# A hybrid attention block on one core: new order with PSUM turns, shared memory and transfers in the planner, and another opening

## The chip, the cores and the metric

The kernel runs on one core of a Trainium2 chip. The metric is the device time of one execution in microseconds (us). A run is one execution; the time of a kernel is the median of its runs.

The engines are PE (TensorE: matrix products and transposes), DVE (VectorE), ACT (ScalarE), POOL (GpSimd) and SP, which issues transfers. Each engine runs its instructions in the order in which they were issued and waits at an instruction whose data isn't there, so the order of the program on each engine decides who waits for whom. PSUM is the memory into which PE writes its results; SBUF is the other memory on the core.

## The reference

One layer, 1024 tokens by 1024 channels, float32. Shift, scale and gate (six vectors of 1024) come from a vector c.

```python
c_act = jax.nn.silu(c)
mod = (c_act @ w_ada[l] + b_ada[l])[:, None, :]
shift1, scale1, gate1, shift2, scale2, gate2 = jnp.split(mod, 6, axis=-1)
h = rms_norm(x, norm1_w[l]) * (1.0 + scale1) + shift1
x = x + gate1 * hybrid_mixer(h, ...)
h = rms_norm(x, norm2_w[l]) * (1.0 + scale2) + shift2
x = x + gate2 * swiglu(h, w_gate[l], w_up[l], w_down[l])
return rms_norm(x, norm_f_w)
```

The mixer projects h by w_in to q, k, v, z of four heads of 128, two columns a and b per head, and the three parts of a short gated convolution. q, k and v pass a causal convolution of width 4 and SiLU; a gated delta rule in chunks of 64 tokens then needs, per chunk, decays from a, the products of k with k and q, a triangular inverse of 64x64, and a chain over the chunks that carries a 128x128 state. The results, gated by z, and the short convolution's go through w_out. SwiGLU has 2816 inner channels.

## The kernel before

**Tiling.** The channels stand on the 128 partitions in eight blocks (k = 0 to 7); the tokens are split into two halves of 512 (hf = 0, 1). Each float32 operand of a large product is split into a high and a low part, and a product is three passes (high by high, low by high, high by low) of 128x128 weights against 512 columns. These are the rows `acc` of the profile. `h` is the normalised input (high and low), `u` a split block of w_in, `whl` one of the first blocks of w_in.

**The opening** works on the first half of the tokens. x is loaded in four tiles (`x0`). The sums of squares are taken by ACT, the roots give `rs`; tiles 0 and 1 are scaled by rs on DVE, while for tiles 2 and 3 the transpose of the first block multiplies by a diagonal `dgx` of rs instead, on PE. `load0` loads, block by block, a block of w_ada's scale and shift (`wa`, 512 KB each) and a block of w_in (`wr`). `sums0` has DVE multiply a block of `wa` with c (`c_bc`, spread over the partitions by PE's products `ps`) and sum along the row; ACT makes the columns `s1c` and `b1c` from the sums. `xh0` transposes x (`tr`); `h_make` writes h's high part from PSUM by ACT, once more in full as `hf`, and DVE subtracts for the low part. `wsplit0` splits `wr`, and `acc0` runs the first products into six PSUM banks. `HEAT` counts dummy products (`heat`), placed ahead of these to keep PE at work: 4 and 12 in the code ahead of the planner and 16 in `acc0`.

**The planner.** From `load0` on, everything up to the middle of the kernel is written as tasks, each a thread of the program that builds the kernel. Class `Sim` runs them: each operation asks for a start, `cost` prices it, `ready` says when its data and places are free, `MARGIN`, `HOLD`, `BIAS` and the table `PR` of priorities weigh, and the operation that can start first is issued next. So the planner's opinion of costs, start times (`T_START`, `PIPE0`) and waits writes the order on each engine. All operations issued through it carry one line of the profile, L452 (`either`); those issued in plain order carry L87 on PE and L88 elsewhere.

**Tasks of the delta rule.** `ab_phase(hf)` makes PE's products `ab`, a copy of them to SBUF (`raw<-ab`), PE's transposes `abt`, then by small DVE and ACT steps the decays, and PE's products `G`. `decays` and `stage_a` make per head the exponentials (`L`, `at`, `WQ`; loaded as `WQ<-g_scr`), PE's transposes `kT` and `qT`, and the products `kk` and `qk`. `gdn(hf)` then solves the triangles on DVE (pairs of operations on tiles `A` and `qs`), copies blocks of the result from `xbd` to `DD` (a tile of tag `qs`) and `XA` (tag `A`), transposes `DD` on DVE, and spawns `merge`, whose first products on PE are `P<-qs,L`, followed by `Q<-qs,A`. The chain has products V, K, A and O per chunk; `output` norms and gates them and PE transposes them (`y<-ident,u`).

**Memory.** The first half's pools (x, s) are given back and used again as pool gp for the delta rule's tiles; b1 is given back and used as x2 for the residual input; `xbd` is used twice. `h1_work` makes the second half's h from the old memory; the tiles of gp wait for it. A first use of such memory waits for the last use of the old. `load_y` (`y0`, `y1`) reloads the mixer's outputs (`raw<-y_scr`) and splits them to `WQ` for w_out's products (`o`). `coordinator` opens the pools and loads the eight tiles of x2; tiles 2 to 7 were either issued at once or held back (`held`) until w_out's weights were loaded.

After the planner's end comes a part in hand-written order: the rest of w_out, SwiGLU (`acc`, L87) and its down projection (`dn`), with the final norm. The change leaves it alone.

Of the kernel before, what the change touches and what calls it, by code (L numbers as in the profile page):

```python
# [9 lines left out]
F32 = mybir.dt.float32  # L10
# [8 lines left out]
HEAT = (4, 12, 16)  # L19
# [32 lines left out]
def kernel(  # L52
# [6 lines left out]
    w_mod: bass.AP,  # L59
    w_in0: bass.AP,  # L60
# [197 lines left out]
    mods = sp.tile([P, 2 * KB], F32, name="mods", tag="mods")  # L258
# [13 lines left out]
    for i, t in enumerate(x0):  # L272
# [4 lines left out]
        seq("dve", DVE.reciprocal(rs, s1))  # L277
        if i < 2:
            seq("dve", DVE.tensor_scalar(t, t, rs, None, ALU.mult))
        elif i == 2:  # L280
            seq("dve", DVE.scalar_tensor_tensor(nb1, bac[:, 8:16], 1.0, n1c, ALU.add, ALU.mult))
            seq("dve", DVE.tensor_scalar(dgx[i], ident, rs, None, ALU.mult))
        else:
            seq("act", ACT.activation(dgx[i], ident, AF.Copy, scale=rs))
# [21 lines left out]
    class Sim:  # L306
        ENG = {"pe": "pe", "dve": "dve", "act": "act", "pool": "pool", "sp": "sp"}

        def __init__(self, chain_, start):
# [5 lines left out]
            self.log, self.idle = [], {}  # L315
# [4 lines left out]
        def own(self, t, res, i, t0=0.0):  # L320
            self.owner[t.tensor.name] = (res, i)
            if t0:
                self.acc[t.tensor.name] = [[0, P, 0, 1 << 30, t0, True, None]]
# [50 lines left out]

        def cost(self, eng, op, a, k):
            outs, ins = [], []
# [21 lines left out]
            elif eng == "act":  # L398
                big = max([n] + [v.free_size() for v in ins])
                busy = 0.15 + (0.1 if hasattr(k.get("scale"), "tensor") else 0.0) + big * 0.0007 + (0.19 if "accum_out" in k else 0.0)  # L400
# [4 lines left out]
            elif eng == "pool":  # L405
                busy = 1.1 if op == "tensor_tensor" else 0.1 + n * 0.0009 if op == "memset" else 0.65 if n >= 256 else 0.5
                lat = busy + 0.15
            else:
# [6 lines left out]
                else:  # L415
                    busy = 0.08 + big * 0.00104 + (0.05 if op == "scalar_tensor_tensor" else 0.0)
# [5 lines left out]
        def ready(self, eng, outs, ins):  # L422
            t = 0.0
            for w, aps in ((True, outs), (False, ins)):
                for ap in aps:
                    name, p0, p1, f0, f1, dram = self.region(ap)
                    for a in self.acc.get(name, ()):
                        if (w or a[5]) and a[0] < p1 and p0 < a[1] and a[2] < f1 and f0 < a[3]:
                            if eng == "pe" and a[6] == "pe" or dram and w or eng == "dma" and w and a[5] and a[6] == "dma":
                                continue  # L430
# [66 lines left out]
        def run(self):  # L497
            while True:
# [25 lines left out]
                if lat is None:  # L524
                    run_ = min(n_ for n_ in (ap.ap[-1][1] * 4 for ap in outs + ins))
                    self.pipe = max(t + DMA_T[0], self.pipe) + outs[0].nbytes() / (150e3 if run_ <= 128 else 290e3 if run_ <= 1024 else 380e3)
                    end = rd = self.pipe + DMA_T[1]
                else:
# [24 lines left out]
    for t, at in [(x0[0], 8.9), (x0[1], 9.8), (x0[2], 7.4), (x0[3], 8.4), (dgx[2], 10.2), (dgx[3], 11.1), (rs0, 10.7)] + [(cols_a, 5.0), (nb1, 9.7), (c_act, 4.0), (c_bc, 7.2)]:  # L553
# [58 lines left out]

    def load0():
        for k in range(KB):
            t = wa[k] = was.tile(wap, [P, 2, D], F32, "wa")
            for s_ in (1, 0):
                dma(t[:, s_], w_mod[k, :, s_])
# [8 lines left out]
    def sums0():  # L626
        cb = c_bc.rearrange("p a b c -> p (a b c)")
        for k in range(KB):
# [3 lines left out]
            for s_, col in ((1, s1c), (0, b1c)):  # L632
                r = mods[:, 2 * k + s_:2 * k + s_ + 1]
                DVE.scalar_tensor_tensor(t[:, s_], t[:, s_], 1.0, cb, ALU.mult, ALU.mult, accum_out=r)
                if s_:
                    ACT.activation(s1c[:, k:k + 1], r, AF.Identity, bias=nb1[:, k:k + 1], scale=n1c[:, k:k + 1])
                else:
                    ACT.activation(b1c[:, k:k + 1], r, AF.Identity, bias=bac[:, k:k + 1])
            free(t)
            done.add(("cols", k))  # L640
# [8 lines left out]
    def xh0():  # L649
        for k in range(KB):  # L650
# [4 lines left out]
            for i in range(4):  # L655
                if k == 0 and i > 1:
# [6 lines left out]
            h = h_slot(k, 0)  # L663
            h_make(k, h, ps, h_hi)
            H[k][0] = h
# [3 lines left out]
    def h_make(k, h, ps, first=None):  # L669
        hf = hfs.tile(sp, [P, HT], F32, "hf")  # L670
        ACT.activation(h[:, 0, :], ps, AF.Identity, bias=b1c[:, k:k + 1], scale=s1c[:, k:k + 1])
# [8 lines left out]
        DVE.tensor_tensor(h[:, 1, :], hf, h[:, 0, :].bitcast(F32), ALU.subtract)  # L680
        free(hf)

    def wsplit0():
        for k in range(KB):
# [4 lines left out]
            w_hi[k] = u  # L689
            DVE.tensor_tensor(u[:, 1, :], wr[k], u[:, 0, :].bitcast(F32), ALU.subtract)  # L690
# [153 lines left out]
    h1_left = list(range(KB))  # L844

    def h1_work():
        sim.wait(lambda: "x1" in done)
        while h1_left:
# [6 lines left out]
            free(hf)  # L855
            H[k][1] = h
# [140 lines left out]
    held, n_wout = [], [0]  # L997

    def ev_o(ps, m):
        sim.wait(lambda: ("x2", m) in done and "g1" in done)  # L1000
# [202 lines left out]
    def gdn(hf):  # L1203
# [40 lines left out]
        DVE.transpose(flat(DD[:, 1]), flat(DD[:, 0]))  # L1244
# [100 lines left out]
    def w_unit(k, ch, take, out_):  # L1345
# [3 lines left out]
        if n_wout[0] == 2 * KB:  # L1349
            done.add("wout")  # L1350
            for kw, m in held:
                seq("sp", nc.sync.dma_start(**kw))
                done.add(("x2", m))
# [28 lines left out]
    def take_lx(n):  # L1382
        def take():
            sim.wait(lambda: all(("uw", 1, h) in done for h in heads))
            if len(xbd) == 1:
                xbd.append(gp.tile([P, 4, HT], F32R, name="wu", tag="xbd", bufs=1))
            return gt("L", (P, HT), F32R), xbd[1][:, n, :]
        return take

    def take_wq():  # L1390
        t = gt("WQ", (P, 2, HT), F32R)
# [20 lines left out]
    def y1():  # L1412
        sim.wait(lambda: ("chain", 1) in done)
# [1228 lines left out]
```

## Time and profile before

| | us |
|---|---|
| median of 3 runs | 1144.19 (1143.35 to 1146.99) |
| the profiled execution | 1145.62 |
| its span | 1143.8 |
| first large product of PE | 15.71 |
| PE busy | 1126.6 |
| DVE busy | 948.6 |
| ACT busy | 612.1 |
| POOL busy | 99.3 |

A row of the waits view names the waiting engine, its operation, the operation that ended last before it, then the sum of the waits in us, their number and the longest. A row of the timeline has start, duration, engine, line, operation, output <- inputs, shapes, and in brackets the idle time of the engine before it with what ended it. Neighbouring equal instructions are gathered in one row (xN). A float32 product of PE is recorded as two passes. In a row of the windows stand the stretch, its length, and the busy time of PE, weight loads, DVE, ACT and POOL, then PE's granted clock, the share of the DMA engines and GB/s.

### The profile page before, as it was taken

What the parts mean: (1) busy time and instruction counts of PE and PEld (TensorE: products, weight loads), DVE (VectorE), ACT (ScalarE), POOL (GpSimd) and SP (SyncE); (2) the same over time, 40 slices, a digit from 0 to 9 for tenths busy, and PEclk for the clock granted to TensorE, in tenths of its full rate; (3) what the DMA queues carried; (4) which work ended last, traced back from release to release, by engine and by line L of the source; (5) the groups of instructions that cost most, each with busy time, mean ns of one, the idle gap of its engine ahead of it and who ended that gap; (6) DMA issues with size and microseconds to landing.
All of it is one profiled execution on the core that took longest, in us unless ns stands there. A gap on an engine that the chain in (4) does not pass through costs nothing.

```text
span 1143.8 us, 17102 instructions
## 1 busy us (share of the span) xinstructions
PE 1126.6 (98%) x5660; PEld 951.2 (83%) x5660; DVE 948.6 (83%) x1909; ACT 612.1 (54%) x1372; POOL 99.3 (9%) x150
## 2 busy tenths in 40 slices
PE   9998999999999999999999999999999999999997
PEld 7887888898888897888888888888888888888885
DVE  7798879889989856699988998878888886689976
ACT  7686863649733643255544544545454476454344
POOL 0010100101100201000010010101010000000302
PEclk9999999999999999999999999999999999999999
DMA  9933256655355472440367667876677599669933
GB/s 367 353 102 102 79 171 192 177 180 183 116 180 174 159 279 68 74 148 19 139 181 210 171 187 177 233 197 162 183 207 200 138 329 362 206 177 355 289 136 147
DMA packets 164978, 214.65 MB, mean 188 GB/s; under 512 B 52589, under 2 KB 81305, under 8 KB 164889
## 3 DMA queue, kind: packets, MB, share of 16 engines
q1 hardware_dynamic: 155832, 198.69, 53.4%
q0 software_dynamic: 7712, 14.42, 8.0%
q8 instruction: 44, 0.72, 0.3%
q10 hardware_dynamic: 1344, 0.46, 0.2%
q14 instruction: 46, 0.37, 0.1%
HBM read 163.94 MB, written 60.58 MB: 196 GB/s over the span
## 4 chain that ended last, share of the span: by engine, by line
PE 90%; ACT 3%; DVE 3%; DMA 1%; issue 1%; POOL 0%; SPq 0%; ACTq 0%; DVEq 0%
PE acc L87 36%; PE acc L452 24%; PE dn L87 16%; PE o L87 4%; PE o L452 3%; DVE xo L88 1%; PE O L452 1%; PE P L452 1%; PE Q L452 1%; PE V L452 1%; PE qk L452 1%; DMA raw<-y_scr 1%; PE K L452 1%; PE A L452 1%; ACT L L452 1%
## 5 line engine op out<-in xcount | busy, mean ns | idle before, releaser
L452 PE MATMUL acc<-h,u 128*128 128x512 f32 x1200 | 293.6, 396 | 0.0
L452 PEld LDWEIGHTS acc<-h,u 128*128 128x128 f32 x1200 | 220.4, 188 | 42.4
L87 PE MATMUL acc<-h,hl 128*128 128x512 f32 (+1 forms) x540 | 109.1, 353 | 0.1
L87 PEld LDWEIGHTS acc<-h,hl 128*128 128x128 f32 x540 | 90.3, 189 | 15.1 <-issue 0.5
L87 PE MATMUL acc<-h,u 128*128 128x512 f32 (+1 forms) x516 | 100.4, 345 | 0.0
L87 PE MATMUL acc<-T,hl 128*128 128x512 f32 x408 | 97.6, 391 | 0.3 <-DVE T L88 0.3
L87 PEld LDWEIGHTS acc<-h,u 128*128 128x128 f32 x516 | 84.7, 189 | 12.6
L87 PE MATMUL acc<-T,u 128*128 128x512 f32 x384 | 91.2, 390 | 0.0
L87 PE MATMUL dn<-h,h 128*128 128x512 f32 x396 | 90.7, 389 | 0.0
L87 PEld LDWEIGHTS acc<-T,hl 128*128 128x128 f32 x408 | 75.2, 188 | 15.8 <-DVE T L88 0.8
L87 PEld LDWEIGHTS dn<-h,h 128*128 128x128 f32 x396 | 74.4, 188 | 15.4
L87 PEld LDWEIGHTS acc<-T,u 128*128 128x128 f32 x384 | 71.0, 188 | 14.1
L452 ACT CAST u<-raw 128x512 fp32r<-128x512 f32 x68 | 41.9, 619 | 53.9 <-PE acc L452 46.5
L452 DVE TENSOR_TENSOR u<-raw,u 128x512 fp32r<-128x512 f32 x82 | 56.6, 692 | 6.4 <-ACT u L452 5.8
L88 ACT COPY L<-acc 128x256 f32<-128x256 f32 x68 | 25.3, 372 | 64.4 <-PE acc L87 64.0
L88 ACT CAST h<-rw 128x512 fp32r<-128x512 f32 x60 | 35.1, 619 | 40.8 <-PE dn L87 26.3
L88 DVE TENSOR_TENSOR xo<-xo,dn 128x512 f32<-128x512 f32 x66 | 44.9, 684 | 14.1 <-PE dn L87 13.6
L452 DVE SCALAR_TENSOR_TENSOR cv<-pr,cols_a,cv 128x512 f32<-128x512 f32 x72 | 53.0, 749 | 1.5 <-ACT cv L452 1.3
L88 DVE TENSOR_TENSOR h<-rw,h 128x512 fp32r<-128x512 f32 x60 | 39.7, 687 | 15.6 <-ACT h L88 15.6
L452 DVE SCALAR_TENSOR_TENSOR raw<-raw,cb 128x512 f32<-128x512 f32 x64 | 43.8, 686 | 4.3 <-DMA raw<-in_w_mod_dram 3.9
L88 DVE TENSOR_TENSOR cc<-cc,acc 128x512 f32<-128x512 f32 x66 | 41.3, 646 | 4.9 <-PE acc L87 4.9
L88 ACT COPY cc<-acc 128x512 f32<-128x512 f32 x64 | 35.2, 585 | 19.0 <-PE acc L87 19.0
(399 smaller groups left out, 2193.0 us busy)
## 6 DMA issues: line engine op xcount, KB each, us to landing
raw<-in_w_in_dram SPq DMA_DIRECT2D x82, 256.0 KB, 3.4
am_scr<-cc SPq DMA_DIRECT2D x75, 256.0 KB, 2.2
raw<-in_w_mod_dram SPq DMA_DIRECT2D x64, 256.0 KB, 3.1
rw<-am_scr SPq DMA_DIRECT2D x53, 256.0 KB, 5.3
R<-in_w_gate_dram SPq DMA_DIRECT2D x22, 512.0 KB, 5.1
R<-in_w_up_dram SPq DMA_DIRECT2D x22, 512.0 KB, 5.9
rw<-bm SPq DMA_DIRECT2D x43, 256.0 KB, 5.3
wa<-in_w_mod_dram SPq DMA_DIRECT2D x16, 512.0 KB, 9.3
```

The source lines that it names most:

```text
L87: return call(*a, **k)
L88: ins = call(*a, **k)
L452: ins = call(*a, **k)
```

## The change

**Opening.** A new input `w_sc0` has the first block's scale weights in w_ada's own layout (512 KB), loaded in plain order right behind x. Eight products of 128x1 on PE (`sc0`, task `scale0`) sum them against c; ACT makes `s1c` of block 0 from PSUM. DVE's reduction of that block and its transfer in `load0` are gone. The first block's shift is loaded and reduced in two halves of 512. Tile 1 of x is scaled by ACT instead of DVE; `dgx` of tile 3 is made by DVE instead of ACT. The first block's h-high is written in two halves, columns 256 to 511 by DVE, then 0 to 255 by ACT; its low part is a task of its own that waits for the reduction of block 1. HEAT goes from (4, 12, 16) to (4, 4, 14).

**Planner.** `ready` lets accesses of different engines to one PSUM bank take turns, and no longer waits for an engine's own earlier write. A transfer's issue waits for the landing of the eighth before it. New costs for strided operands, POOL, ACT. MARGIN of PE is 1.0 (was 0.6). `gone` says when the old memory of gp, x2 and xbd is free.

**Tasks.** `take_wq` waits for the second chain, `y1` for w_out's weights; tiles 2 to 7 of x2 wait for w_out's weights or for the output product of their turn. In `gdn` the transpose of DD is issued ahead of POOL's copies to XA.

```diff
-HEAT = (4, 12, 16)
+HEAT = (4, 4, 14)
-T_START = (8.6, 10.5, 11.1, 2.9, 2.9)
-PIPE0 = 8.25
+T_START = (8.6, 10.05, 11.7, 2.9, 3.4)
+PIPE0 = 9.2
-MARGIN = dict(pe=0.6)
+MARGIN = dict(pe=1.0)
...
+    wsc0 = xp.tile([P, D], F32, name=nm("wsc0"), tag="x", bufs=8)
...
+    seq("sp", SP.dma_start(out=wsc0, in_=w_sc0))
...
+                        if ap.space == PSUM and a[6] not in (eng, None):
+                            t = max(t, a[4])
+                            continue
...
-                at = way[2] = self.ready("dma" if lat is None else eng, outs, ins) + MARGIN.get(eng, 0.0)
+                at = way[2] = max(self.ready("dma" if lat is None else eng, outs, ins) + MARGIN.get(eng, 0.0), 0.0 if lat else self.landed[-8])
...
+    def scale0():
+        ps = bank(chb, "sc0")
+        for kk in range(KB):
+            mm(ps[:, 0:1], wsc0[:, kk * P:(kk + 1) * P], c_act[:, kk:kk + 1], kk == 0, kk == KB - 1)
+        ACT.activation(s1c[:, 0:1], ps[:, 0:1], AF.Identity, bias=nb1[:, 0:1], scale=n1c[:, 0:1])
+        free(ps)
+        done.add("scale0")
...
+            if k == 0:
+                a, b = slice(0, 256), slice(256, HT)
+                DVE.tensor_scalar(h[:, 0, b], ps[:, b], s1c[:, 0:1], b1c[:, 0:1], ALU.mult, ALU.add)
+                done.add("hi0")
+                ACT.activation(h[:, 0, a], ps[:, a], AF.Identity, bias=b1c[:, 0:1], scale=s1c[:, 0:1])
...
+        DVE.transpose(flat(DD[:, 1]), flat(DD[:, 0]))
         for p in range(2):
             for c in range(2):
                 q, m, r = 64 * c + 32 - 32 * p, Q_AT[p, c], 64 * c
                 POOL.tensor_copy(XA[q:q + 32, :, m:m + 32], xbd[0][r:r + 32, p::2, r:r + 32])
-        DVE.transpose(flat(DD[:, 1]), flat(DD[:, 0]))
...
     def take_wq():
+        sim.wait(lambda: ("chain", 1) in done)
...
     def y1():
-        sim.wait(lambda: ("chain", 1) in done)
+        sim.wait(lambda: "wout" in done)
...
+        left = sim.gone(x1t + h1_t)
+        for res in GP.values():
+            res.slots = [(max(t0, left), i) for t0, i in res.slots]
...
-            if i < 2 or "wout" in done:
-                dma(x2[m], x_t[m])
-                done.add(("x2", m))
-            else:
-                sim.op("sp", "dma_start", lambda **kw: held.append((kw, m)) or [], (), dict(out=x2[m], in_=x_t[m]))
+            if i > 1:
+                sim.wait(lambda: "wout" in done or len(begun) >= i)
+            dma(x2[m], x_t[m])
+            done.add(("x2", m))
```

The order on three engines at three places. First PE from its start to the first large products, before (x is a tile of the input, tr the transposed first block, ps the spread of c):

```order
L87 MATMUL ps_206<-raw_204,ones 128x512
L87 MATMUL heat<-ident,ones 128x128 x12
L452 MATMUL heat<-ident,ones 128x128 x5
L452 MATMUL tr_272<-ident,x_184 128x128
L452 MATMUL heat<-ident,ones 128x128 x3
L452 MATMUL tr_272<-ident,x_185 128x128
L452 MATMUL heat<-ident,ones 128x128
L452 MATMUL tr_272<-dgx_228,x_186 128x128
L452 MATMUL heat<-ident,ones 128x128 x3
L452 MATMUL tr_272<-dgx_229,x_187 128x128
L452 MATMUL heat<-ident,ones 128x128 x4
L452 MATMUL acc_252<-h_0_110_316,whl_278 128x512
```

The same place after the change:

```order
L88 MATMUL ps_208<-raw_206,ones 128x512
L88 MATMUL heat<-ident,ones 128x128 x4
L468 MATMUL heat<-ident,ones 128x128 x8
L468 MATMUL tr_265<-ident,x_184 128x128
L468 MATMUL heat<-ident,ones 128x128 x3
L468 MATMUL sc_103_264<-c_act,wsc_85_188 128x1 x8
L468 MATMUL tr_265<-ident,x_185 128x128
L468 MATMUL tr_265<-dgx_222,x_186 128x128
L468 MATMUL tr_265<-dgx_223,x_187 128x128
L468 MATMUL heat<-ident,ones 128x128 x3
L468 MATMUL acc_244<-h_0_112_315,whl_271 128x512
```

Seventeen heats stand ahead of the first transpose before and twelve after; the products of the scale stand between the first transpose and the second, and the other transposes follow without heats between them.

Second, ACT at the second half's ab, before (WQ and L are the first exponentials of the decays, u a split weight):

```order
L452 ACTIVATE h_1_275_1178<-hf_1179,b1c 128x512
L452 ACTIVATE h_1_271_1156<-hf_1157,b1c 128x512
L452 CAST u_1217<-raw_1194 128x512
L452 ACT_TABLE_LOAD
L452 ACTIVATE WQ_1254<-WQ_1254 128x512
L452 ACTIVATE L_1246<-L_1246,G_1090 128x128
L452 COPY raw_1284<-ab_1236 128x512
```

And after:

```order
L468 CAST u_1192<-raw_1167 128x512
L468 ACTIVATE h_1_277_1180<-hf_1181,b1c 128x512
L468 COPY ch_1194<-acc_1135 128x512
L468 ACTIVATE vT_1206<-cv_1158 128x512
L468 COPY raw_1274<-ab_1229 128x512
L468 ACT_TABLE_LOAD
L468 ACTIVATE WQ_1247<-WQ_1247 128x512
```

The copy of ab has moved from behind the table load and two exponentials to ahead of them. On PE ten products stand between the last ab and the four abt after the change, eight before; G follows forty-four products later than before.

Third, DVE ahead of the second half's P, before (qs is the tile that is transposed, the others are weight splits, a reduction of w_ada and a convolution):

```order
L452 TENSOR_TENSOR h_0_803_4136<-raw_4130,h_0_803_4136 128x512
L452 TENSOR_TENSOR cv_4163<-acc_4152,cv_4163 128x512
L452 COPY qs_4212<-xbd 32x256
L452 TENSOR_TENSOR u_4215<-raw_4171,u_4215 128x512
L452 SCALAR_TENSOR_TENSOR raw_4146,msum<-raw_4146,cb_1827 128x512
L452 TENSOR_TENSOR h_0_812_4198<-raw_4190,h_0_812_4198 128x512
L452 STREAM_TRANSPOSE qs_4212<-qs_4212 128x256
```

And after:

```order
L468 STREAM_TRANSPOSE turn<-A_3711 64x512
L468 TENSOR_TENSOR u_4185<-raw_4147,u_4185 128x512
L468 SCALAR_TENSOR_TENSOR cv_4169<-ch_4102,cols_a,cv_4169 128x512
L468 TENSOR_TENSOR h_0_804_4137<-raw_4130,h_0_804_4137 128x512
L468 TENSOR_TENSOR cv_4169<-acc_4159,cv_4169 128x512
L468 TENSOR_TENSOR u_4208<-raw_4189,u_4208 128x512
L468 TENSOR_TENSOR h_0_806_4145<-raw_4139,h_0_806_4145 128x512
L468 STREAM_TRANSPOSE qs_4223<-qs_4223 128x256
```

DVE's own copy into qs is gone (all four copies are on ACT). From the last kk to P, PE has 243 products in the first half after the change and 250 before, and 261 against 266 in the second.

More of the change, by code (lines that the diff above doesn't have):

```diff
@@ L59 @@
     w_mod: bass.AP,
+    w_sc0: bass.AP,
     w_in0: bass.AP,
@@ L282 @@
             seq("dve", DVE.tensor_scalar(dgx[i], ident, rs, None, ALU.mult))
-        else:
-            seq("act", ACT.activation(dgx[i], ident, AF.Copy, scale=rs))
+        elif i == 3:
+            seq("act", ACT.activation(x0[1], x0[1], AF.Copy, scale=rs0[:, 1:2]))
     accs = {m: psp.tile([P, HT], F32, name=nm("acc"), tag=f"b{i}") for i, m in enumerate(heads01)}
@@ L373, in region, with gone @@
             return name, p0, p0 + dims[0][1], lo, hi + 1, ap.space == bass.MemoryType.DRAM
+        def gone(self, aps):
+            return max([a[4] for ap in aps for a in self.acc.get(ap.tensor.name, ())] + [self.now])
         def cost(self, eng, op, a, k):
+            apart = lambda ap, n: n >= 256 and ap.space != PSUM and abs(ap.ap[-1][0]) > 1 and ap.ap[-1][1] > 1
             outs, ins = [], []
@@ L399, in cost @@
                 big = max([n] + [v.free_size() for v in ins])
-                busy = 0.15 + (0.1 if hasattr(k.get("scale"), "tensor") else 0.0) + big * 0.0007 + (0.19 if "accum_out" in k else 0.0)
+                busy = 0.15 + 0.09 * sum(hasattr(k.get(n_), "tensor") for n_ in ("scale", "bias")) + big * 0.0007
+                busy += (0.06 if n <= P else 0.19) if "accum_out" in k else 0.3 if apart(ins[0], n) else 0.0
                 lat = busy + 0.25
@@ L415, in cost @@
                 else:
-                    busy = 0.08 + big * 0.00104 + (0.05 if op == "scalar_tensor_tensor" else 0.0)
+                    busy = 0.08 + big * 0.00104 + (0.05 if op in ("scalar_tensor_tensor", "tensor_scalar") else 0.0)
+                if op == "transpose" and apart(ins[0], n):
+                    busy += n * 0.00104
                 if "accum_out" in k:
@@ L527, in run @@
                     end = rd = self.pipe + DMA_T[1]
+                    self.landed.append(end)
                 else:
@@ L631, in sums0 @@
             t = wa[k]
[L632 to L638, printed above, removed]
+            made = []
+            for s_ in (1, 0) if k else (0,):
+                for c in halves_of(k):
+                    r = mods[:, 2 * k + s_:2 * k + s_ + 1] if c.stop == D else mods[:, 2 * KB:2 * KB + 1]
+                    DVE.scalar_tensor_tensor(t[:, s_, c], t[:, s_, c], 1.0, cb[:, c], ALU.mult, ALU.mult, accum_out=r)
+                    made.append(r)
+            done.add(("sum", k))
+            if k:
+                ACT.activation(s1c[:, k:k + 1], made.pop(0), AF.Identity, bias=nb1[:, k:k + 1], scale=n1c[:, k:k + 1])
+            add = bac[:, k:k + 1]
+            for r in made:
+                to = b1c[:, k:k + 1] if r is made[-1] else mods[:, 2 * KB + 1:2 * KB + 2]
+                ACT.activation(to, r, AF.Identity, bias=add)
+                add = to
             free(t)
+            sim.wait(lambda: "scale0" in done)
             done.add(("cols", k))
@@ L655, in xh0 @@
             for i in range(4):
+                if k == 0 and i == 3:
+                    sim.wait(lambda: "dgx3" in done)
                 if k == 0 and i > 1:
@@ L670, in h_make @@
         hf = hfs.tile(sp, [P, HT], F32, "hf")
-        ACT.activation(h[:, 0, :], ps, AF.Identity, bias=b1c[:, k:k + 1], scale=s1c[:, k:k + 1])
+        if k:
+            ACT.activation(h[:, 0, :], ps, AF.Identity, bias=b1c[:, k:k + 1], scale=s1c[:, k:k + 1])
         if first is not None:
@@ L679, in h_make, with low @@
         free(ps)
-        DVE.tensor_tensor(h[:, 1, :], hf, h[:, 0, :].bitcast(F32), ALU.subtract)
-        free(hf)
+        def low():
+            if k == 0:
+                sim.wait(lambda: ("sum", 1) in done)
+            DVE.tensor_tensor(h[:, 1, :], hf, h[:, 0, :].bitcast(F32), ALU.subtract)
+            free(hf)
+            H[k][0] = h
+        if k == 0:
+            sim.spawn(low, 0.2)
+        else:
+            low()
     def wsplit0():
@@ L1386, in take @@
                 xbd.append(gp.tile([P, 4, HT], F32R, name="wu", tag="xbd", bufs=1))
+                sim.acc[xbd[1].tensor.name] = [[0, P, 0, 1 << 30, sim.gone(xbd[:1]), True, None]]
             return gt("L", (P, HT), F32R), xbd[1][:, n, :]
```

48 lines of the change are left out of this document (31 added, 17 removed).

## The prediction

> **What bounds the kernel now.** I read the page's parts 1 and 2 first, then the waits of TensorE (PE), then windows, then the timeline at each wait.
>
> ```profile
> PE 1126.6 (98%) x5660; PEld 951.2 (83%) x5660; DVE 948.6 (83%) x1909; ACT 612.1 (54%) x1372; POOL 99.3 (9%) x150
> PEclk9999999999999999999999999999999999999999
> ```
> PE is busy 98% of the 1143.8 us span at full granted clock. No other engine comes near, so only time in which PE stands idle can be won, or work taken from it. The waits view lists that idle time by releaser (total, times, longest):
>
> ```profile
> PE abt L452 <- ACT raw L452: 3.6, 2, 3.4
> PE P L452 <- DVE qs L452: 1.7, 1, 1.7
> PE heat L87 <- POOL ident masks.py:199: 1.4, 1, 1.4
> PE y L452 <- DVE u L452: 1.2, 2, 1.0
> PE G L452 <- ACT jk L452: 0.7, 1, 0.7
> PE ps L87 <- DVE raw L88: 0.7, 1, 0.7
> ```
> The windows (length, PE busy, PEld, DVE, ACT, POOL busy) say in which stage it lies:
>
> ```profile
> 15.70:111.00 95.30, 94.24 (x430) 76.81 (x430) 82.61 (x172) 71.26 (x122) 8.09 (x11) 1.00 0.61 218
> 111.00:139.00 28.00, 24.47 (x139) 20.40 (x140) 23.07 (x80) 25.81 (x89) 2.85 (x6) 1.00 0.31 95
> 139.00:400.00 261.00, 259.31 (x1385) 221.61 (x1384) 230.20 (x624) 147.23 (x436) 28.20 (x45) 1.00 0.54 167
> 400.00:560.00 160.00, 158.38 (x764) 130.75 (x763) 118.97 (x209) 68.94 (x140) 5.92 (x5) 1.00 0.40 119
> 560.00:1114.00 554.00, 554.00 (x2778) 472.65 (x2776) 464.38 (x779) 276.36 (x535) 44.64 (x56) 1.00 0.74 215
> ```
> Length less PE busy is 1.06, 3.53, 1.69, 1.62 and 0: 7.9 us between the first product at 15.7 and 1114. That is the most that new waits and orders can win there. Of it the waits view names abt 3.6 + P 1.7 + y 1.2 + G 0.7 = 7.2. The second half (560 on), which the change leaves alone, has nothing to win.
>
> **The change part by part.** (Line numbers are those of before.)
>
> *Opening.* PE's rows there with DVE's reduction (wa) and ACT's h, then the nearest ones for what is new (the last five: 128x1 products; DVE and ACT reading one PSUM tile, 128 columns each; ACT at 256 columns):
>
> ```profile
> 11.20 1.28 PE L452 MATMUL heat<-ident,ones 128*128 128x128 f32 x10
> 12.12 1.22 DVE L452 SCALAR_TENSOR_TENSOR wa<-wa,c_bc 128x1024 f32<-128x1024 f32 x1
> 12.32 0.27 PE L452 MATMUL tr<-ident,x 128*128 128x128 f32 x1
> 12.43 0.83 PE L452 MATMUL heat<-ident,ones 128*128 128x128 f32 x6
> 14.32 0.39 PE L452 MATMUL tr<-dgx,x 128*128 128x128 f32 x2
> 14.81 0.78 ACT L452 ACTIVATE h<-tr,b1c,s1c 128x512 fp32r<-128x512 f32 x1 [1.13 <-PE tr L452]
> 15.71 1.17 PE L452 MATMUL acc<-h,whl 128*128 128x512 f32 x4
> 470.26 0.79 PE ss L87 x8
> 155.63 0.35 DVE L452 TENSOR_SCALAR u<-vT,bv 128x128 f32<-128x128 f32 x1 [0.53 <-ACT u L452]
> 156.01 0.37 ACT L452 ACTIVATE u<-vT,bv 128x128 f32<-128x128 f32 x1 [0.42 <-DVE u L452]
> 156.41 0.35 DVE L452 TENSOR_SCALAR u<-vT,bv 128x128 f32<-128x128 f32 x1 [0.43 <-ACT u L452]
> L88 ACT COPY L<-acc 128x256 f32<-128x256 f32 x68 | 25.3, 372 | 64.4 <-PE acc L87 64.0
> ```
> A heat is two passes of 0.11 us. Ten heats fewer are 2.2 us of PE time, but they fill time in which PE would wait. The chain: the first transpose can start at 11.20 instead of 12.32, where five heats stood. Behind it three heats (0.67) and eight 128x1 products; "ss" is four such (eight passes) in 0.79, so 1.58. Then three transposes of five passes, 0.55: the last ends its start-to-start at 11.20 + 0.11 + 0.67 + 1.58 + 0.55 = 14.1, against 14.54 before. Half of h-high by DVE and half by ACT follow. The vT rows show the two engines at one tile by turns, each waiting for the other; the new order has the same, ACT's half waiting for DVE's. By turns: DVE 256 columns is above 0.35 (128 columns), about 0.46; ACT 256 is above 0.37 (the plain copy), about 0.50; 0.96 against the 0.78 of the one ACT pass. The first product comes 0.4 earlier and 0.2 later: about 0.2 won; I take 0.1, since the next products need the second block at the old time. Bounds: 0.9 won (if the halves lay side by side and all three heats were dead time) to 0.3 lost (sc0 at heat price, 1.79, and both halves 0.05 dearer). DVE's 1.22 us reduction of the scale and its DMA go, hidden work either way.
>
> The Trainium skill ("PSUM — Partial Sum Buffer", "PSUM bank collisions raise a hardware error") says that two engines must not touch one bank and partition quadrant at once, ACT with VectorE included, so they have to be kept apart; the vT rows agree. It speaks against halving this eviction: without it the halves would end 0.46 sooner, near the upper bound.
>
> *The wait of abt, second half.*
>
> ```profile
> 104.49 1.42 DVE L452 SCALAR_TENSOR_TENSOR h<-hf,b1c,h 128x512 fp32r<-128x512 f32 x2 [0.88 <-ACT h L452]
> 106.06 3.31 DMA WQ<-g_scr
> 110.85 1.28 ACT L452 ACT_TABLE_LOAD   x1 [5.27 <-DVE at L452]
> 112.97 0.56 ACT L452 COPY raw<-ab 128x512 f32<-128x512 f32 x1
> 113.59 0.66 PE L452 MATMUL abt<-ident,raw 128*128 128x128 f32 x4 [3.41 <-ACT raw L452]
> 373.66 5.60 PE L452 MATMUL acc<-h,u 128*128 128x512 f32 x24
> ```
> PE needs ab transposed; ACT's copy raw<-ab stands behind a table load and two exponentials, and these wait for a load of decays that is issued only at 106.06, when h1_work's last DVE operation has freed the memory. In the new order the copy stands ahead of the table load, needing ab alone, and PE has 10 products (0.23 each: 5.60 by 24) in place of 8 before abt: 2.3 us of cover against the copy's 0.56. The 3.4 goes; of the first half's abt (the other 0.2) too, as its copy moves to DVE under 16 products instead of 11. G moves 44 products later, 10 us: its 0.7 goes. What comes due next is the same stage: ACT is 25.81 busy of 28 there, 92%. The new order asks for the transposed q 0.7 to 2.8 us later than the old, so I put new small waits at 0.5 to 1 us, 0.8.
>
> *P.* The transpose qs of both halves, ahead of P:
>
> ```profile
> 208.17 0.43 DVE L452 STREAM_TRANSPOSE qs<-qs 128x256 f32<-128x256 f32 x1
> 209.15 1.95 PE L452 MATMUL P<-qs,L 128*128 128x128 f32 x16
> 377.67 0.44 DVE L452 COPY qs<-xbd 32x256 f32<-32x256 f32 x1
> 380.46 0.43 DVE L452 STREAM_TRANSPOSE qs<-qs 128x256 f32<-128x256 f32 x1
> 380.95 2.05 PE L452 MATMUL P<-qs,L 128*128 128x128 f32 x16 [1.69 <-DVE qs L452]
> ```
> In the second half qs is complete at 378.11 but transposed at 380.46, behind three DVE operations. The new order puts all four copies on ACT and the transpose right behind: 2.35 earlier. But from the last kk (which feeds the solve) to P PE now has 261 products against 266, 1.15 us less; of 1.69 there remains about 0.3 (1.69 - 2.35 + 1.15 = 0.5, less 0.2 as a copy leaves DVE). In the first half no wait stands in the trace, slack 209.15 - 208.60 = 0.55; 243 products against 250 take 1.6 away, the transpose comes 0.7 to 1.4 earlier: a new wait of 0 to 1.5, taken at 0.4. P wins 1.7 - 0.3 - 0.4 = 1.0.
>
> *y.*
> ```profile
> 424.90 1.83 SPq L452 DMA_DIRECT2D raw<-y_scr  x4
> 431.36 0.43 DVE L452 CAST WQ<-raw 128x512 fp32r<-128x512 f32 x1 [2.06 <-DMA raw<-y_scr]
> 435.68 0.66 PE L452 MATMUL y<-ident,u 128*128 128x128 f32 x4 [1.05 <-DVE u L452]
> ```
> DVE's norm of the last outputs stood behind a cast that waited for these loads, which SP issued behind eight loads of x2. Now six of the eight wait for w_out, two of the four y loads are issued ahead, and 30 output products stand before y. The 1.2 goes. x2 is needed only from the first output products on; a late tile costs DVE, not PE, while PSUM has free banks.
>
> Sum: opening 0.1, abt 3.6, G 0.7, stage A -0.8, P 1.0, y 1.2: 5.8 us. The profiled execution took 1145.62 (span and 1.82 around it), 1.43 over the median of 1144.19; from it 1139.8, from the median **1138.4**. About 0.3% (3.4 us) is what a measurement of this kernel can tell from no change: faster means below 1140.8, slower above 1147.6.
>
> **The rivals.**
> *A: the wait only moves.* ACT paces stage A (111 to 139), so PE, freed from abt, stands later at kk, kT or qT. For it: 92% ACT. Against: PE's order has other products to fill, and DVE (23.07 of 28) can help. ACT then starts earlier by 0 to 0.7 (one of the two h operations of 104.49 is gone from that place), taken at 0.5; with 0.2 from the first abt, the stage gives 0.7 instead of 3.5. Sum 0.7 + 0.1 + 1.0 + 1.2 = 3.0: 1141.2, within 0.3%.
> *B: slower, the solve becomes the bound.* Both halves have fewer products between kk and P, and the triangular solve between is a chain of dependent DVE operations with others set between them. If the new mixture delays it, PE waits at P one for one. Slower by 0.3% takes 5.8 + 3.4 = 9.2 us over two solves: some seven more foreign DVE operations of 0.7 (the two h above: 1.42) in each. The order shows 28 between in the first, as before, which speaks against.
> *C: the opening does not do what it says.* The scale's products or the two turns cost what the reduction gave: -0.3 instead of 0.1, 1138.8; still faster.
> *D: the clock cools.* With ten heats fewer, PE may fall back to the slow passes with which it began:
>
> ```profile
> 7.79 3.57 PE L87 MATMUL heat<-ident,ones 128*128 128x128 f32 x24
> ```
> These 24 passes take 3.57 where 24 at 0.11 are 2.6: about the first seven or eight ran at 0.21, until 9.4, so PE was slow for some 5 us after the ps products began at 4.22. A second such stretch at half speed costs 2.6: gain 3.2, 1141.0. Against: the abt row after 3.41 idle is 0.66 long, the y row after 1.05 idle the same, so that much idle did not cool it, and the opening has under 1 us by the chain above. The Trainium skill ("TensorE: Matmul & The Clock Gate", Part 1) halves the clock after an idle window of about 3.4 us; the abt row, at that length, shows no halving.
>
> **How the numbers follow.** Forecast 0.52; A 0.24; B 0.08; C 0.08; D 0.02; other small waits that leave it within 0.3% 0.02, other slower 0.04. Faster: 0.52 + 0.08 = 0.60. Same: 0.24 + 0.02 + 0.02 = 0.28. Slower: 0.08 + 0.04 = 0.12. Low end: all of the 7.9 and 0.9 of the opening, 8.8: 1135.4, rounded down to 1135.0. High end: A with the stage at 0.2, P at 1.7 - 0.3 - 1.5 = -0.1, the opening at -0.3, y at 1.2: 1.0, 1143.2; with a part of the slower cases 1144.0.
>
> **What would show it.** In the waits of PE the rows abt, G and y gone; P at most 0.8; no new row over 1 us (kk, kT or qT: then A; a P row of several us: B). ACT's copy raw<-ab right behind ab's last product, ahead of the table load. First product at 15.5 to 15.75, the eight sc0 products in 1.4 to 1.8. The window 111 to 139 with under 1.5 us of PE idle. Wrong it would be if the idle sum from first product to the tail stays over 5 us, or the tail past 1114 grows.

## The result and the profile after

| kernel | median, us | before beside it | ratio, 95% interval |
|---|---|---|---|
| after | 1135.48 (1135.19 to 1136.64, 6 runs) | 1144.85 (6 runs) | 0.9918 [0.9905, 0.9930] |
| after, run again (e9) | 1135.59 (1134.91 to 1136.11, 5 runs) | 1143.73 (9 runs) | 0.9925 [0.9911, 0.9939] |

The change makes the kernel faster by 8.1 to 9.4 us, where 5.8 was forecast. The profiled execution of after took 1135.19 with a span of 1133.4; that is 10.4 under before's profiled one, about 1 more than the medians differ by.

The waits of PE in after (what waits, on what, then the sum in us, the number, the longest):

```profile
core 0 of [0], span 1133.4 us
PE heat L88 <- POOL eps_c L89: 1.5, 1, 1.5
PE acc L468 <- ACT h L468: 0.9, 1, 0.9
PE sT L468 <- POOL rs L468: 0.7, 1, 0.7
PE sc L468 <- DMA wsc<-in_w_sc_dram: 0.5, 1, 0.5
PE acc L88 <- DVE T L89: 0.3, 1, 0.3
```

All of abt, P, y and G are gone. Three rows are new: sc and the first acc lie in the opening, sT (the transposed row norms, at 62.2) is in the middle. The windows of after, over the same stages (stretch, its length, PE busy, then the other engines):

```profile
14.26:111.00 96.74, 96.08 (x440) 78.59 (x441) 87.81 (x185) 71.40 (x122) 7.78 (x11) 1.00 0.63 227
111.00:139.00 28.00, 28.00 (x160) 24.01 (x159) 22.85 (x69) 26.75 (x97) 4.16 (x7) 1.00 0.30 85
139.00:400.00 261.00, 261.00 (x1403) 224.00 (x1402) 225.69 (x624) 151.74 (x446) 28.25 (x44) 1.00 0.55 171
400.00:560.00 160.00, 159.64 (x759) 131.95 (x759) 125.41 (x216) 68.63 (x139) 5.64 (x5) 1.00 0.40 122
```

Length less PE busy is 0.66, 0, 0 and 0.36: 1.0 us in place of 7.9. The stage from 111 to 139, with 3.53 idle before, has none, though ACT is busier there than before (26.75 of 28). The places of the four old waits, in after's timeline:

```profile
106.54 0.59 ACT L468 COPY raw<-ab 128x512 f32<-128x512 f32 x1 [3.63 <-issue]
108.51 1.28 ACT L468 ACT_TABLE_LOAD   x1 [1.38 <-DVE at L468]
108.57 0.60 PE L468 MATMUL abt<-ident,raw 128*128 128x128 f32 x4
129.97 0.60 PE L468 MATMUL qT<-ident,qkT 128*128 128x128 f32 x4
201.55 0.44 DVE L468 STREAM_TRANSPOSE qs<-qs 128x256 f32<-128x256 f32 x1
203.59 1.95 PE L468 MATMUL P<-qs,L 128*128 128x128 f32 x16
371.72 0.45 DVE L468 STREAM_TRANSPOSE qs<-qs 128x256 f32<-128x256 f32 x1 [0.18 <-ACT qs L468]
373.39 1.95 PE L468 MATMUL P<-qs,L 128*128 128x128 f32 x16
430.42 0.60 PE L468 MATMUL y<-ident,u 128*128 128x128 f32 x4
```

The copy is done at 107.13 and abt starts at 108.57. Both transposes qs end ahead of P, by 1.6 us in the first half and by 1.2 in the second. PE's rows carry no idle time in brackets: nothing here waits.

The last group of dn starts at 1132.21 before and at 1122.17 after, 10.04 apart. The first large product came at 15.71 and at 14.26, so 1.45 of that was there at the start and 8.6 arose between. Of the 8.6 the windows show 6.9 as idle time. The other 1.7 is in no row of any wait. PE starts the same number of instructions in both kernels there (5585). Measured against the median step of their shape, their starts lie 7.8 us further apart in sum before, and 6.1 after, waits left out; 0.75 of the difference lies in the stage from 111 to 139. So there are fewer products that start a little late behind the one before; what delays them is not shown.

```profile
1132.21 4.67 PE L87 MATMUL dn<-wu,wu 128*128 128x512 f32 x18
```

```profile
14.26 0.73 PE L468 MATMUL acc<-h,whl 128*128 128x512 f32 x2 [0.89 <-ACT h L468]
1122.17 4.64 PE L88 MATMUL dn<-wu,wu 128*128 128x512 f32 x18
```

### The profile page after: what moved, and what is told of

It is laid out like the page before. It is cut to its first block, busy times and chain, and to the rows that moved or that the text cites. A ratio compares the mean times of both kernels' runs of the same rounds, so it can differ in the third digit from the quotient of the medians.

```text
span 1133.4 us, 17102 instructions
## 1 busy us (share of the span) xinstructions
PE 1122.7 (99%) x5656; PEld 950.3 (84%) x5656; DVE 943.9 (83%) x1902; ACT 614.3 (54%) x1381; POOL 100.1 (9%) x150
## 4 chain that ended last, share of the span: by engine, by line
PE 91%; DMA 4%; DVE 2%; ACT 1%; issue 1%; SPq 0%; POOL 0%; ACTq 0%; DVEq 0%
PE acc L88 36%; PE acc L468 24%; PE dn L88 17%; PE o L88 4%; PE o L468 4%; DMA wa<-in_w_mod_dram 2%; PE O L468 1%; DVE xo L89 1%; DMA x<-in_x_dram 1%; PE V L468 1%; PE kk L468 1%; PE qk L468 1%; PE Q L468 1%; PE P L468 1%; DMA xt<-in_x_t_dram 1%
## 5 line engine op out<-in xcount | busy, mean ns | idle before, releaser
L468 ACT CAST u<-raw 128x512 fp32r<-128x512 f32 x61 | 37.5, 619 | 48.0 <-PE acc L468 43.8
```

What stands on the lines that cost most here:

```text
L468: ins = call(*a, **k)
```

## The experiments

One unit of 0.001 in a ratio is 1.14 us. The kernel after has two ratios, 0.9918 and 0.9925 (e9), so a comparison with it through the kernel before beside each gives two numbers.

| experiment | median | before beside it | ratio, 95% interval |
|---|---|---|---|
| e1 before, 8 heats fewer | 1144.66 | 1144.44 | 1.0001 [0.9992, 1.0010] |
| e2 after, 8 heats more | 1137.60 | 1144.44 | 0.9940 [0.9926, 0.9954] |
| e3 before, copy of ab first | 1142.74 | 1144.44 | 0.9987 [0.9979, 0.9996] |
| e4 after, first h whole | 1135.80 | 1144.44 | 0.9927 [0.9914, 0.9939] |
| e5 after, memory not told | 1140.74 | 1145.02 | 0.9960 [0.9946, 0.9973] |
| e6 before, margin 1.0 | 1141.32 | 1145.02 | 0.9969 [0.9959, 0.9978] |
| e7 after, margin 0.6 | 1137.66 | 1145.02 | 0.9938 [0.9924, 0.9952] |
| e8 after, no turns | 1141.79 | 1145.02 | 0.9974 [0.9965, 0.9983] |
| e10 after, h whole, sT later | 1137.16 | 1143.73 | 0.9935 [0.9923, 0.9948] |
| e11 after, margin 1.4 | 1140.48 | 1143.73 | 0.9968 [0.9955, 0.9980] |
| e12 e10 with a wide scale | 1134.40 | 1143.90 | 0.9916 [0.9902, 0.9929] |

In e3, e4, e10 and e12 the planner decides as in the kernel they start from, and only what is named is issued elsewhere; so every other instruction keeps its place. In e5 to e8 and e11 the planner writes a new order.

### The one move: the copy of ab (e3)

Cut from the edit, whose other lines issue every operation as it comes:

```diff
...
+            if eng == "act" and call.__name__ == "copy" and a[1].tensor.name.startswith("ab_"):
+                self.n_ab += 1
+                self.emit1(eng, call, a, k)
+                if self.n_ab == 2:
+                    for one in self.kept:
+                        self.emit1(*one)
+            elif eng == "act" and call.__name__ == "activation" and self.n_ab == 1 and out.startswith(("WQ", "L_")):
+                self.kept.append((eng, call, a, k))
...
```

> The kernel before with one move on one engine: ACT's copy of the second half's ab stands ahead of the table load and the first two exponentials, all other orders as they were. Theory (PE idle time is time): the 3.4 us wait of abt goes and no later wait takes its place, time -3.4 us. Rival A of the prediction (ACT paces the stage, the wait moves to kk, kT, qT or G): -0.7 us or less.

Measured: 0.9987, 1.5 us faster [0.5, 2.4], between the two. The waits of PE:

```profile
PE qk L455 <- ACT kt L455: 1.2, 1, 1.2
PE qT L455 <- DVE at L455: 0.8, 1, 0.8
PE G L455 <- ACT jk L455: 0.7, 1, 0.7
PE kT L455 <- DVE L L455: 0.7, 1, 0.7
PE abt L455 <- ACT raw L455: 0.2, 1, 0.2
PE y L455 <- DVE u L455: 0.2, 1, 0.2
```

abt's long wait is gone, as the theory had it, but 1.2 + 0.8 + 0.7 = 2.7 us of it stand again at qk, qT and kT, which had none of this before. That is rival A, for this one move: PE comes to the stage's products earlier, and ACT and DVE are not ready. 0.7 of the 3.4 is left as a gain. In this profile the row y, which the move doesn't touch, is also 0.2 where before has 1.2. The first qT of this kernel, with its wait:

```profile
129.76 0.66 PE L455 MATMUL qT<-ident,qkT 128*128 128x128 f32 x4 [0.79 <-DVE at L455]
```

In after it comes at 129.97, without a wait: the same pace, but PE has 72 products between abt and that qT where this order has 50. What after gains here is not that qT comes sooner but that PE does 22 more products (5 us) in the meantime. No run changes this count alone, so that it is the count which decides is argued from the three orders and not shown.

### Which rule did it (e5 to e8, e11)

```diff
-            return max([a[4] for ap in aps for a in self.acc.get(ap.tensor.name, ())] + [self.now])
+            return 0.0
```

> The kernel after with gone() answering 0: the planner is not told when reused memory becomes free, all else as after. Theory (the time is set by how many products PE has between the steps of the delta rule): the new order has 225 products from the last kk of the first half to P against 243 after, 18 x 0.23 = 4.1 us less, of which the kernel after had 1.6 in hand, so a wait of about 2.5 us at P; and 415 products ahead of the first qT against 429, a wait of up to 3 us in stage A. Time +2.5 to +5.5 us over the kernel after. Rival (the other rules carry the gain): 0 to 1.

Measured: 0.9960, 4.0 to 4.8 us slower than after by its two ratios. The size is the theory's, the place is not: there is no wait at the first half's P or at qT. PE waits 1.1 at the second half's P and 1.0 at the transpose of the gates, sT:

```profile
PE P L468 <- DVE qs L468: 1.1, 1, 1.1
PE sT L468 <- DVE mod_c L468: 1.0, 1, 1.0
```

These are two of the 4.0 to 4.8. In the profiled runs of e5, e7, e8 and e11 the granted clock also fell to 0.5 for 3.4 us in the opening (shown below for e4), which can cost half of that, 1.7 us, on top of the waits.

```diff
-MARGIN = dict(pe=0.6)
+MARGIN = dict(pe=1.0)
```

> The kernel before with one number changed, PE's margin 1.0 instead of 0.6; opening, rules and tasks as before. Theory (products between the steps decide, whatever rule put them there): ACT's copy of ab stands ahead of the table load here too, 434 products stand ahead of the first qT (before 410, after 429), 453 ahead of the second G (428, 472), so the 3.4 us of abt, the 0.7 of G and no new wait in stage A: -3 to -5 us. Rival (the told rules are needed; the margin alone is noise): 0 to -1.

Measured: 0.9969, 3.5 us faster [2.5, 4.7], within the theory's -3 to -5. One number, on the kernel before, gives over a third of the size of the change's gain. But not "no new wait": abt and G have no row any more, and smaller ones have come in the stage and later.

```profile
PE P L452 <- DVE xbd L452: 1.0, 2, 0.6
PE qk L452 <- DVE kt L452: 0.7, 1, 0.7
PE P L452 <- DVE qs L452: 0.7, 1, 0.7
PE vT L452 <- DVE L L452: 0.7, 1, 0.7
PE y L452 <- DVE u L452: 0.6, 1, 0.6
```

```diff
-MARGIN = dict(pe=1.0)
+MARGIN = dict(pe=0.6)
```

> The kernel after with PE's margin back at 0.6, all else as after. Theory: 225 products from the last kk of the first half to P against 243, 1.6 in hand: a wait of about 2.5 us at P; stage A has 424 products ahead of the first qT against 429, within 1.2 us. Time +2.5 to +3.5. Rival (the margin does nothing once the rules are told): 0 to 0.5.

Measured: 0.9938, 1.5 to 2.3 us slower than after by its two ratios. The wait that was forecast at P did not come; the one wait after the opening that after did not have is 0.4 at a later P (of the second half). The slowness of the profiled run (span 1136.7 against 1133.4) is for the most part its opening: the first product at 15.82, and the slow clock around it. Whether the margin itself costs anything here is left open.

```diff
-                        if ap.space == PSUM and a[6] not in (eng, None):
-                            t = max(t, a[4])
-                            continue
```

> The kernel after without the rule that engines take turns at a PSUM bank, all else as after. Theory: 217 products from the last kk of the first half to P against 243, 6.0 us less with 1.6 in hand: a wait of about 4.4 us at P; stage A has 431 ahead of the first qT, no wait there. Time +4 to +5. Rival (turns matter only for the planner's own clock, not for the waits): 0 to 1.

Measured: 0.9974, 5.6 to 6.4 us slower than after by its two ratios. Again no wait at P<-qs; instead many small ones:

```profile
PE Q L465 <- ACT PP L465: 0.8, 2, 0.6
PE abt L465 <- ACT raw L465: 0.8, 1, 0.8
PE G L465 <- DVE g L465: 0.8, 1, 0.8
PE Q L465 <- DVE xbd L465: 0.6, 1, 0.6
```

The theory as I had put it, a fixed pace of the solve against a count of products, fell in three cases of three: the likely reason, not tested, is that with the order of DVE new as well the solve ends at another time. What stands is that e5 and e8 have orders with small waits spread over the kernel, beyond what the clock explains.

```diff
-MARGIN = dict(pe=1.0)
+MARGIN = dict(pe=1.4)
```

> The kernel after with PE's margin 1.4 instead of 1.0. Theory (more margin, more products between the steps, fewer waits): first qT 80 products behind abt (after: 72), 244 products from the last kk to P (243): no wait over 1 us, time -0.5 to +0.5 us against the kernel after run beside it. Rival (1.0 is a chance find among re-plannings; any other number brings waits back, as 0.6 did): +1.5 to +3.

Measured: 0.9968 against 0.9925 for the unchanged kernel beside it, 4.9 us slower: the rival, and more. In its opening the first product waits for h, and abt and gT wait again:

```profile
PE acc L468 <- ACT h L468: 2.4, 1, 2.4
PE abt L468 <- ACT raw L468: 1.2, 1, 1.2
PE gT L468 <- DVE gpad L468: 0.8, 1, 0.8
```

So 1.0 is a value found for this order, not a direction in which more is better. The fall of the clock in this profile comes behind the wait of 2.4.

### The heats (e1, e2)

```diff
-HEAT = (4, 12, 16)
+HEAT = (4, 4, 16)
```

> The kernel before with 8 of the 12 heats ahead of the planner left out, the order otherwise as it was. Theory (the heats stood on the path: the chain of before is PE alone from ps at 4.22 to the first product at 15.71): the last transpose comes 1.8 earlier, h then waits for the shift's column at 13.67 instead of starting at 14.81, so the first product comes about 1.1 earlier and the time falls by about 1.1 us. Rival (the prediction's words: the heats fill time in which PE would wait): first product and time unchanged, 0.

Measured: 1.0001, no difference, at most 0.9 us won. The first product of the profiled run came at 14.19, after a wait of 1.5, so PE no longer holds it up; yet a y wait of 1.1 us stands at 269.1, where before had none:

```profile
PE abt L452 <- ACT raw L452: 2.6, 2, 2.4
PE y L452 <- DVE u L452: 1.7, 3, 1.1
```

In time the rival is right. Where the earlier start went is not shown: abt's wait is 1.0 shorter than before's, so the four rows abt, P, y and G sum to 6.7 against 7.2, and the profiled run (1143.62) is itself 1.0 under its median. y's row also shows how a wait differs between kernels with one order there: 1.2 before, 1.7 here, 0.2 in e3.

```diff
-HEAT = (4, 4, 14)
+HEAT = (4, 12, 14)
```

> The kernel after with the 8 heats put back ahead of the planner, the order otherwise as it is. Theory (heats on the path): the scale's products start 1.05 later than at 10.16, the rest of the opening with them, so the first product comes about 0.9 later than 14.26 and the time rises by about 0.9 us over the kernel after. Rival (heats fill waiting, the opening is bound by transfers): 0 to 0.2.

Measured: 0.9940, 1.7 to 2.5 us slower than after's two ratios: the theory, and twice its size. The products of the scale (sc) and with them the column s1c now come late, and h waits for PE:

```profile
12.49 1.84 PE L468 MATMUL sc<-c_act,wsc 128*128 128x1 f32 x16
14.34 0.61 PE L468 MATMUL tr<-dgx,x 128*128 128x128 f32 x4
15.06 0.54 DVE L468 TENSOR_SCALAR h<-tr,s1c,b1c 128x256 fp32r<-128x256 f32 x1 [0.77 <-PE tr L468]
```

So the heats that before could bear cannot stand ahead of the scale on PE: in after they had to go.

### The halves, the spread and the clock (e4, e9, e10, e12)

```diff
-                DVE.tensor_scalar(h[:, 0, b], ps[:, b], s1c[:, 0:1], b1c[:, 0:1], ALU.mult, ALU.add)
+                sim.op("dve", "tensor_scalar", lambda *a_, **k_: [], (h[:, 0, b], ps[:, b], s1c[:, 0:1], b1c[:, 0:1], ALU.mult, ALU.add), {})
                 done.add("hi0")
-                ACT.activation(h[:, 0, a], ps[:, a], AF.Identity, bias=b1c[:, 0:1], scale=s1c[:, 0:1])
+                sim.op("act", "activation", lambda *a_, **k_: nc.scalar.activation(h[:, 0, :], ps, AF.Identity, bias=b1c[:, 0:1], scale=s1c[:, 0:1]),
...
```

The planner books both halves as it does for after; what is issued is nothing on DVE and the whole block on ACT.

> The kernel after with the first block's h-high written whole by ACT instead of half by DVE and half by ACT in turn, all orders otherwise as they are. Theory (the halves cost 0.54 + 0.56 in turn against 0.78): first product 0.3 to 0.4 earlier, time -0.3 us. Rival (what follows the first products is bound by the transfers and DVE): the gain is given back at the next block, 0. Rival (halving wins): +0.3 us.

Measured: 0.9927, no difference from after. One ACT pass takes 0.78 where the two halves take turns, 0.54 and 0.56; but something else gave it back, as the windows of one us each show (granted clock is the third number from the end):

```profile
13.00:14.00 1.00, 1.00 (x10) 0.85 (x8) 0.96 (x2) 0.68 (x2) 0.00 (x0) 1.00 1.04 416
14.00:15.00 1.00, 0.74 (x3) 0.56 (x3) 1.00 (x2) 1.00 (x3) 0.00 (x0) 0.76 1.01 396
15.00:16.00 1.00, 1.00 (x4) 0.76 (x3) 1.00 (x3) 1.00 (x2) 0.00 (x0) 0.50 1.02 400
17.00:18.00 1.00, 1.00 (x5) 0.70 (x4) 0.62 (x2) 1.00 (x3) 0.00 (x0) 0.54 1.02 406
```

The clock fell to half from 14.5 to 17.9, over the first products. The times of the five executions go with their mean clock: 1136.4 twice at 0.997, 1134.63 and 1134.88 at 0.999. So where the clock held, the whole block may well be the better one.

> The kernel after, unchanged, for the spread. Theory (the first product of the profiled runs moves with the clock and the landing of the first loads, not with the change): ratio to before 0.990 to 0.9935 as measured at first, first product anywhere from 14.2 to 15.8, PE idle between it and the down projection 1.5 us or less. Rival (the 1.45 us by which the first product came earlier in the two profiles is the change's): first product within 0.2 of 14.26.

Measured (the kernel after, no edit): 0.9925, first product at 14.58. The first product thus moved by 0.3 us between two runs of one kernel; that of e3, whose opening is before's, came at 14.88 against 15.71. By these four the opening wins between 0.3 and 1.45. Part of the 1.45 is likely chance: by the clock records of the traces PE's clock rose to full speed at 9.3 us in before's profile, at 5.1 in e3's, at 4.8 in after's and at 7.0 in e9's. The sT wait of 0.7 did not come again.

e10 adds to e4 that PE issues sT later. Five were meant; the count stops one short, and sT comes four products later (176 in place of 172 large products ahead of it):

```diff
...
+            if eng == "pe" and call.__name__ == "transpose" and out.startswith("sT_") and not self.left:
+                self.kept.append((eng, call, a, k))
...
+            if eng == "pe" and self.kept:
+                self.left += 1
+                if self.left > 5:
+                    self.emit1(*self.kept.pop())
...
```

> The kernel after with the first block's h-high whole on ACT and the transpose sT (of the row norms) five products later on PE; all other orders as they are. Theory (idle time of PE is time): the 0.66 at sT goes, the first product comes 0.3 earlier, -1.0 us against the kernel after run beside it. Rival (given back, or under what can be measured): 0.

Measured: 0.9935 against 0.9925 beside it, no gain, rather 1.1 slower. The wait of sT has no row, but e9 without the edit had none either. The first product came at 14.20, 0.4 earlier than in e9, and then again at half the clock:

```profile
14.20 1.12 PE L471 MATMUL acc<-h,whl 128*128 128x512 f32 x2 [0.26 <-ACT h L729]
15.40 2.48 PE L471 MATMUL acc<-h,whl 128*128 128x512 f32 x5
```

Five products in 2.48 where after has 1.41 for five. e12 is e10 with wide products in the scale's places:

```diff
-            mm(ps[:, 0:1], wsc0[:, kk * P:(kk + 1) * P], c_act[:, kk:kk + 1], kk == 0, kk == KB - 1)
+            sim.op("pe", "matmul", lambda *a_, **k_: nc.tensor.matmul(ps[:, 0:P], wsc0[:, kk * P:(kk + 1) * P], c_act[:, kk:kk + 1].to_broadcast([P, P]), **k_),
...
```

> The kernel of e10 with the eight products of the first block's scale fed 128 equal columns (the one column of c repeated) instead of one, in the same places; the answer is read from the first column. Theory (eight products of one column leave the array idle though PE counts as busy, so the granted clock falls to 0.5 for some 3 us behind them, as in e4 and e10 from 14.2 on): clock 1.0 from 14 to 18, 1.3 to 1.6 us back against e10, ratio to before about 0.992. Rival (the clock falls for its own reasons, the width does nothing): clock 0.5 there again, ratio 0.9935 as e10. Also possible: the wide products are slower than 1.84 for the eight, and what the clock gives is paid there.

Measured: 0.9916, 2.2 us better than e10 by the ratios, its five runs within 0.6 us (1134.20 to 1134.82). The eight wide products take 2.02 where the narrow ones take 1.84 to 1.92; the passes start 0.11 apart in both, so the difference lies at the first and the last. And the clock holds:

```profile
14.00:15.00 1.00, 0.71 (x5) 0.57 (x5) 1.00 (x2) 1.00 (x3) 0.00 (x0) 1.00 1.01 407
15.00:16.00 1.00, 1.00 (x7) 0.84 (x6) 1.00 (x3) 1.00 (x2) 0.00 (x0) 1.00 1.04 418
```

The mean clocks of the single executions agree: 0.998 or 0.999 in all five of e12, 0.995 in three of e10's five. e12 ran on another chip than e10, each against the kernel before on its own chip. It has the lowest median of all, 1134.40; by the ratios that is 0.2 to 1.0 us below after, within its interval.

## Why the prediction was right, and where its sizes were off

**What bounds the kernel** was read rightly: only idle time of PE could be won, and the waits view named where. 6.9 of the 7.9 us of idle time that the windows showed were won.

**abt, G and y** (3.6 + 0.7 + 1.2) went, as the sum had it. But the step from "the copy stands ahead of the table load" to "The 3.4 goes" was only half a reason: e3 does just that, the wait at abt goes, and 2.7 of it stand again at qk, kT and qT. In after nothing comes back, and there the order puts 22 more products before the first qT. The prediction had these counts for abt and for G and did not count them for kT and qT, where it saw only that the order "asks for the transposed q 0.7 to 2.8 us later" and booked that as a risk. The same delay is the likely cover. The 1.2 of y was read off one execution: in e1 and e3, with before's order there, it is 1.7 and 0.2.

**Stage A, -0.8**: the mis-sized term, measured 0 (28.00 busy of 28). **P, 1.0**: measured 1.7; neither residual came, since the transposes had 1.6 and 1.2 us in hand. Against 1.6 (first half) and 1.15 us (second) of cover lost I had set too small a head start of the transposes. The 1.5 that the range took for the first half's new wait is also more than its own terms give: 1.6 lost less the slack of 0.55 is 1.05.

**The opening, 0.1**: measured between 0.3 and 1.45, not settled closer. The halves took turns and cost 0.54 + 0.56, a little over the estimate of 0.96. The heats "fill time in which PE would wait": for before, e1 finds no time in them; ahead of the scale's products e2 finds 1.7 to 2.5 us. The sign "First product at 15.5 to 15.75" failed (14.26 and 14.58). The chain took PE alone as what sets the pace, from an execution of before whose clock rose late; in after PE waited 0.55 us for the scale's weights and 0.89 for h. The bounds don't follow from their own terms either: 0.2 + 0.46 + 0.67 is 1.3 won, not 0.9, and 0.2 - 0.21 - 0.10 is 0.1 lost, not 0.3.

**What was not in the sum**: 1.7 us between the products that no wait's row shows, and the sT wait of 0.7, against. With one exception the misses point the same way, to a larger gain. So the time came out near the low end of the range, and that it lies inside is in part luck: the low end allowed 8.8 us of gain, and the kernel before that ran beside was 9.4 us slower. It had a median of 1144.85 there, 0.66 above the one from which the range was counted.

**The rivals.** A (the wait moves) is what happens to the one move, not to the change. B (the solve) did not come. C did not. D was given 0.02, for a second slow stretch through ten heats fewer and idle time ahead of it; the clock did fall, in the profiles of six kernels made from after, though in neither profile of after itself, and e2 with eight of the heats back is slower. The argument against D, that 3.41 us of idle time did not cool the clock, held for one execution only (last section).

Which of the planner's rules made the gain is not settled: the margin alone gives 3.5 on before, and on after the rule on memory is worth 4.0 to 4.8 and that on turns 5.6 to 6.4, each less up to 1.7 for the clock, and each time by other waits. The new costs, the waits of the tasks `y1` and `take_wq`, the transfers of x2 and the earlier place of the transpose were not tried alone.

## What to carry to other kernels

A wait that is removed by one move can come back at the next steps of the same stage, as in e3, unless the bound engine has other work to put in between: count the instructions between each step and the next, not only at the wait. A planner's constant is tuned to one order; re-measure it in both directions after every rule, since a neighbouring value can cost as much as the rule wins. And compare two profiles only after running one kernel twice: here the first product alone moved by 0.3 and 0.8 us between two runs with one opening.

## What the runs showed of the hardware

Behind the eight float32 products of one column (1.84 us, PE counted busy all the time) the granted clock fell to 0.5 for 3.4 us in both kernels with the whole block (e4, e10); with 128 columns in the same places (e12) it held 1.0. The clock records of the traces say when. In all six profiles with such a fall it began 6.82 or 6.83 us after the clock had first risen (in e11 10.24), and lasted 3.41 or 3.42. These are two (three) steps of 3.41, so the clock was decided at fixed steps counted from its rise. The table has, for the last step of 3.41 us ahead of the fall, or for the step that holds most of the scale's products where none fell, how long these products took in it and how long PE was idle, in us:

| run | clock rises at | scale's products | idle | clock in the next step |
|---|---|---|---|---|
| e4 | 7.68 | 1.66, narrow | 0.26 | 0.5 |
| e10 | 7.50 | 1.74, narrow | 0.26 | 0.5 |
| e5 | 5.51 | 1.75, narrow | 0.60 | 0.5 |
| e7 | 6.74 | 1.92, narrow | 0.90 | 0.5 |
| e8 | 5.38 | 1.88, narrow | 0.41 | 0.5 |
| e11 | 6.96 | none | 2.43 | 0.5 |
| e11, one step earlier | 6.96 | 1.84, narrow | 0.00 | 1.0 |
| e9 | 7.03 | 1.92, narrow | 0.00 | 1.0 |
| e2 | 7.26 | 1.60, narrow | 0.00 | 1.0 |
| after | 4.76 | 1.43, narrow | 0.55 | 1.0 |
| e12 | 5.92 | 2.01, wide | 0.50 | 1.0 |

So the narrow products alone did not bring the fall (e9, e2, the earlier step of e11); together with 0.26 to 0.90 us of idle time in the same step they did in five of six, and idle time of 2.43 us alone did in e11. The wide ones with 0.50 did not. In the four profiles with before's opening (before, e1, e3, e6), which has no such products, the clock held, with up to 1.60 us idle in a step there (e3). That the width makes the difference fits all of these, but e12 is one kernel, and when the clock rises differs from run to run.

By the same steps, counted on from 9.32, the 3.41 us of idle time at abt in before's profile fall into two, with 1.54 and 1.87, and the clock held. In another execution they need not fall so. Of the 61 executions of before beside e1 to e12, 18 have a mean clock of 0.996 or less (median time 1145.70, the others 1144.12); of the 21 of e3 and e6, which lack this wait, none, and one of 11 of after. (A mean also counts the low clock behind the last product, where it costs nothing.) So part of what the change wins may be clock and not waiting; no trace of before shows such a fall, so this is open.

The Trainium skill ("TensorE: Matmul & The Clock Gate", Part 1) ties the slow clock to an idle window of about 3.4 us. The length of the fall agrees with one such window; its cause does not, for in the 3.41 us ahead of e4's fall PE was idle for 0.26, and ahead of e11's for 2.43.
